# A hybrid decoder layer on one core: weight sums, row sums and sample sums of the feed-forward part put elsewhere

## The chip, the cores and the metric

The kernel runs on one core of a Trainium2 chip. The time is that of the device, in microseconds (us), of one execution; three executions of the kernel before took 2315.43, 2320.51 and 2323.57 us, so the median is 2320.51. The engines are named as in the profile: PE (matmuls), DVE (vector), ACT (activations), POOL (general), and SP, which here issues the transfers.

## The reference, cut to what matters

One decoder layer on 2048 prompt rows and 8 x 8 sample rows of 1024 features, in float32. The change touches its second half:

```python
mix = jnp.einsum('bte,ed->btd', jnp.concatenate([attn, gla_out], axis=-1), w_out)
x = x + rms_norm(mix, g_mix_post)
h = rms_norm(x, g_ffn_pre)
u = jax.nn.relu(jnp.einsum('btd,df->btf', h, w_up))      # 1024 -> 4096
f = jnp.einsum('btf,fd->btd', u * u, w_down)             # 4096 -> 1024
x = x + rms_norm(f, g_ffn_post)
```

The first half, the projections, the windowed attention and the gated linear attention, is the same in both kernels.

## The kernel before

Every float32 product is made of three matmuls: each operand is split into a high half (a rounding copy, on ACT) and a low half (the difference, on DVE), and high x high, high x low and low x high are summed in PSUM. The functions `split_by`, `split_up`, `split_sums` and `split_h` make such pairs.

The two feed-forward products are done by seven block products instead of eight (a Strassen-Winograd scheme over 2 x 2 blocks). One operand's blocks are summed over rows, the other's over weights: `H[1]` to `H[7]` are the pieces of the normed rows, and the weights' sums are made per chunk. A piece of 1024 rows is called `sb` (0 or 1); `up(g, before)` is one of 32 chunks (`g`; 0 to 15 for sb 0, 16 to 31 for sb 1) of 256 columns of `w_up`, and in it `p` is the product (1, 5, 7, 6, 3, 2, 4), where 0, 8 and 9 stand for the sample rows' matmuls in sb 0. In a chunk, `raw0` and `raw1` hold the weights as loaded, `w00`/`w01` and `w10`/`w11` their high and low halves, `t13` the weight sums, `s130`/`s131` and `s240`/`s241` the halves of the sums for products 5, 7 and for 6, 3. `sums_13` and `sums_24` each make two sums in `t13`. The products land in four PSUM banks, X (`ua`), Z (`uc`), Y (`ub`) and V (`ud` or `ue` in turn), and are combined into the seven slots of a tile `st` on DVE; ACT squares them (`squared`) and SP stores the tile in `s_d`. `end()` is the part of a chunk's combination that runs during the next chunk. `both` is ACT's copy of the sample rows' result, `fold` a matmul that adds its two halves.

Before the first chunk stands the out projection (line 1237), row block by row block in the order `B_ORDER`, whose last two are blocks 11 and 15. `residual` normalizes such a block, adds it to x, normalizes again, transposes (`xnT`), and for every pair of blocks makes the rows' sums (`ht`), which go through `h_d` in DRAM and come back as the pieces H (`fetch_h`). It is a generator: each `run(res, 1)` lets it go one step further at the place where that stands.

The feed-forward part has no scheduler: the order written in the code is the order of each engine (`ac`, `dv`, `te` and `sy` are wrappers that keep it, all their instructions being recorded at line 138). So a step that waits holds everything behind it on its engine.

Beside the chunks run sums of `w_down`'s blocks for the down projection (`load_down`, `sum_down`, at the places in `SUM_AT`, on DVE, stored in `t_d`). The down projection (`dn`) then reads `s_d` and `t_d` back as `os` and `ot`, splits them, and adds the banks of each product to `f` on DVE (`gather`); `gather_sample` does that for the sample rows (`dsam`, `fs`).

Of the kernel before, what the change touches and what calls it, by code (L numbers as in the profile page):

```python
# [52 lines left out]
SUM_AT = sorted([(g, 1) for g in range(1, NG) if not NFC - 3 < g <= NFC] + [(g, 4) for g in (18, 21, 24, 27)])  # L53
# [95 lines left out]
def hybrid_step_kernel(ctx: ExitStack, tc: tile.TileContext, I, O):  # L149
# [1184 lines left out]
    xsT = U["xs"].tile([P, KT, 2 * NS], F32R, tag="x", name="xsT", bufs=1)  # L1334
    open_pools(R, ("x",), "o")
# [13 lines left out]
    def load_x(i, sync=nc.sync):  # L1349
# [16 lines left out]
    def residual(i, banks, scalar=nc.scalar, vector=nc.vector, tensor=nc.tensor, sync=nc.sync, kinds=None):  # L1366
        n = rows(i)
        last = i in B_ORDER[-2:]
        x = res_x.pop(i, None) or load_x(i)[0]
        ssq = ends[B_ORDER.index(i) % 2]  # L1370
        pool, tag, bufs = (hs_pool, "h1", 1) if last else (R["x"], "x1", 2)
        x1 = pool.tile([P, D], F32, tag=tag, name=f"x1_{i}", bufs=bufs)
# [27 lines left out]
        if i < NB and not second and i:  # L1400
            sums_place(sb, j)
        for h in range(2):
# [8 lines left out]
            if i == NB:  # L1411
                split_copy(xsT[:, kk, :NS], xsT[:, kk, NS:], pt[:, :, :NS], vector)
                continue
            ht = sums[sb, j]
            scalar.activation(ht[:, (6, 2)[h] if second else h], pt, AF.Copy)
            if sb == 0 and not second:
                split_copy(H[h + 1][0][:, :, q], H[h + 1][1][:, :, q], pt, vector)
        yield
        if i == NB or not second:
            return  # L1420
# [55 lines left out]
    def sums_on(g):  # L1476
        return nc.gpsimd if g in (1, NFC, NFC + 1) else dv

    def sums_13(g):
# [3 lines left out]
        sums_on(g).tensor_tensor(t[:, :, 0], a21, a22, op=ALU.add)  # L1483
        sums_on(g).tensor_tensor(t[:, :, 1], a11, a21, op=ALU.subtract)

    def sums_24(g):
# [3 lines left out]
        sums_on(g).tensor_tensor(t[:, :, 0], t[:, :, 0], a11, op=ALU.subtract)  # L1490
        sums_on(g).tensor_tensor(t[:, :, 1], a12, t[:, :, 0], op=ALU.subtract)
# [17 lines left out]
    close_pools(R)  # L1509
    open_pools(U, ("sam", "s13h", "t13", "s13l", "s24h"), "u")  # L1510
    sums_13(0)
    split_sums(0, 13)
    sums_24(0)
# [14 lines left out]
    open_pools(U, ("s24l",), "u")  # L1528
    fetch_h(0, 5)
    fetch_h(0, 7)  # L1530
    run(res)
    fetch_h(0, 6)
    s_first = U["st0"].tile([P, 7, BT], F32, tag="st", name="st_0", bufs=1)
# [3 lines left out]
    load_up(1)  # L1537
# [449 lines left out]
```

## Time and profile before

| | before |
|---|---|
| median of three executions | 2320.51 us |
| profiled execution | 2319.51 us |
| its span in the trace | 2317.7 us |
| granted clock of TensorE, mean | 0.987 |
| PE / DVE / ACT / POOL busy | 96% / 69% / 52% / 13% |
| chain that ended last: PE / DVE / ACT | 71% / 16% / 6% |

A line of busy time names the engine, the operation, the tile written and the tiles read, and behind a bracket the idle time before it with what ended it. A window's line has the stretch in us, its length, the busy time of PE, of its weight loads, of DVE, ACT and POOL with the number of instructions in brackets, then the granted clock, the share of the DMA engines and GB/s. A line of waits has the engine, what it was about to do, what it waited for, the total in us, how often, and the longest. In the profile the out projection runs from 800 to about 976 us, the chunks to about 1655, and the down projection after that.

### The profile page before, as it was taken

The numbers are of one execution on the slowest core, as the hardware profiler recorded it, in microseconds if no ns is written. First come the engines' busy times: TensorE is split into PE (matmuls) and PEld (weight loads), VectorE is DVE, ScalarE is ACT, GpSimd is POOL, SyncE is SP. The second block draws the span as 40 slices with busy tenths as digits, with TensorE's granted clock in tenths as the row PEclk, the third lists the DMA queues.
The fourth block names the chain that finished last, engine by engine and source line by source line (L and its number), as shares of the span: only waits on it lengthen the run. The fifth ranks groups of instructions, "written<-read, shape, count | busy, mean of one in ns | idle before, by whom it ended". The sixth has DMA issues, their size and how long they took to land.

```text
span 2317.7 us, 34065 instructions
## 1 busy us (share of the span) xinstructions
PE 2224.0 (96%) x11800; PEld 1885.6 (81%) x11800; DVE 1609.6 (69%) x3331; ACT 1210.2 (52%) x2513; POOL 290.1 (13%) x440
## 2 busy tenths in 40 slices
PE   8999999999998899979999989999999999999997
PEld 7888887888887788858888878888888887888886
DVE  5888868787777666677677687777644555855557
ACT  5787755444554444445555565555444434554445
POOL 3566412111121101010000010000000000000000
PEclk9999999999999999989999999999999999999999
DMA  7343232121112355765545476666665755876665
GB/s 229 120 152 124 98 94 72 65 71 47 51 47 73 133 179 181 228 220 200 188 169 198 171 260 214 222 231 220 211 205 168 234 182 158 275 231 222 218 193 198
DMA packets 227266, 391.34 MB, mean 169 GB/s; under 512 B 22945, under 2 KB 134966, under 8 KB 223110
## 3 DMA queue, kind: packets, MB, share of 16 engines
q1 hardware_dynamic: 227094, 389.17, 50.0%
q8 instruction: 93, 1.52, 0.3%
q14 instruction: 79, 0.65, 0.1%
HBM read 254.56 MB, written 135.59 MB: 168 GB/s over the span
## 4 chain that ended last, share of the span: by engine, by line
PE 71%; DVE 16%; ACT 6%; issue 3%; DMA 2%; POOL 1%; DVEq 0%; SPq 0%; ACTq 0%; POOLq 0%
PE dn L138 25%; PE uc L138 7%; PE ua L138 7%; PE out L1237 7%; PE gproj L138 5%; PE ue L138 4%; PE ud L138 4%; PE ub L138 3%; DVE s L138 2%; PE proj L138 2%; DVE XQ L973 2%; PE sam L138 1%; PE dsam L138 1%; DVE pl L138 1%; PE gm L138 1%
## 5 line engine op out<-in xcount | busy, mean ns | idle before, releaser
L138 PE MATMUL dn<-ot,os 128*128 128x512 f32 x2688 | 625.0, 390 | 5.0 <-DVE f L138 2.9
L138 PEld LDWEIGHTS dn<-ot,os 128*128 128x128 f32 x2688 | 505.0, 188 | 114.5 <-DVE ot L138 4.7
L138 DVE TENSOR_TENSOR os<-os 128x512 fp32r<-128x512 f32 x224 | 154.7, 691 | 222.5 <-ACT os L138 221.7
L138 PE MATMUL gproj<-wg,gx 128*128 128x388 f32 x1408 | 289.3, 352 | 0.0
L138 ACT ACTIVATE os<-os 128x512 fp32r<-128x512 f32 x224 | 141.4, 631 | 281.1 <-DMA os<-s_d 218.9
L138 PEld LDWEIGHTS gproj<-wg,gx 128*128 128x128 f32 x1408 | 246.7, 192 | 13.5 <-issue 13.1
L138 ACT ACTIVATE st<-st 128x512 f32<-128x512 f32 x224 | 141.2, 630 | 141.9 <-DVE st L138 137.8
L138 PE MATMUL uc<-H,s 128*128 128x512 f32 x768 | 186.1, 391 | 2.0 <-ACT st L138 1.2
L138 PE MATMUL ua<-H,w 128*128 128x512 f32 x744 | 179.9, 390 | 0.9 <-DVE w L138 0.5
L138 PEld LDWEIGHTS uc<-H,s 128*128 128x128 f32 x768 | 144.7, 189 | 32.9 <-ACT st L138 1.7
L138 PEld LDWEIGHTS ua<-H,w 128*128 128x128 f32 x744 | 138.9, 188 | 30.1 <-DVE w L138 1.0
L138 DVE TENSOR_TENSOR st<-st 128x512 f32<-128x512 f32 x160 | 111.0, 694 | 69.4 <-ACT st L138 66.1
L1237 PE MATMUL out<-wo,mt 128*128 128x512 f32 x656 | 155.1, 395 | 3.3 <-DVE x L1387 3.3
L1237 PEld LDWEIGHTS out<-wo,mt 128*128 128x128 f32 x656 | 122.1, 188 | 30.9 <-issue 3.5
L214 POOL TENSOR_TENSOR frs<-rs_v,half 128x1 f32<-128x1 f32 (+1 forms) x13 | 9.0, 689 | 904.5 <-DVE rs_v L138 904.5
L138 ACT ACTIVATE s<-t 128x1024 fp32r<-128x1024 f32 x64 | 67.8, 1060 | 65.6 <-PE ue L138 26.6
L138 DVE TENSOR_TENSOR ot<-ot 128x512 fp32r<-128x512 f32 x128 | 88.2, 689 | 14.7 <-ACT ot L138 13.6
L138 PE MATMUL proj<-wa_hi,xh 128*128 128x384 f32 (+1 forms) x272 | 95.7, 355 | 0.9 <-ACT wa_hi L138 0.6
L138 DVE TENSOR_TENSOR s<-t,s 128x1024 fp32r<-128x1024 f32 x64 | 78.4, 1225 | 25.8 <-ACT s L138 22.5
L138 PE MATMUL proj<-wa_lo,xh 128*128 128x384 f32 (+1 forms) x272 | 94.3, 351 | 0.0
L138 PE MATMUL proj<-wa_hi,xl 128*128 128x384 f32 (+1 forms) x272 | 93.3, 347 | 0.0
L138 ACT ACTIVATE ot<-ot 128x512 fp32r<-128x512 f32 x128 | 80.7, 631 | 20.5 <-DMA ot<-t_d 16.9
(371 smaller groups left out, 4092.2 us busy)
## 6 DMA issues: line engine op xcount, KB each, us to landing
os<-s_d SPq DMA_DIRECT2D x224, 256.0 KB, 2.8
s_d<-st SPq DMA_DIRECT2D x31, 1792.0 KB, 9.0
raw<-in_w_up SPq DMA_DIRECT2D x64, 512.0 KB, 5.5
ot<-t_d SPq DMA_DIRECT2D x128, 256.0 KB, 3.7
rt<-in_w_down SPq DMA_DIRECT2D x96, 256.0 KB, 3.0
t<-in_w_down SPq DMA_DIRECT2D x64, 256.0 KB, 3.4
t_d<-t SPq DMA_DIRECT2D x32, 512.0 KB, 7.2
gx<-xt_d SPq DMA_DIRECT2D x28, 512.0 KB, 4.0
```

Of the source, the lines that this page charges most:

```text
L138: ins = call(*a, **k)
L214: nc.gpsimd.tensor_tensor(out, v[:n], e, op=ALU.pow)
L973: nc.vector.tensor_tensor(xq[rr, :, l, r, : n // 2].rearrange("p g (m b) -> p g m b", b=b), dr[rr], qr[rr], op=ALU.mult)
L1237: te.matmul(p_, x, w[:, cc], start=k + u == 0, stop=k == KT - 1 and u == len(products) - 1)
```

## The change

- **Chunk 0's weight sums.** They were made after the last pair's first block, in `t13`. Now they are made during the out projection, in place of the raw weights, four operations, and the halves for products 5 and 7 with them; the halves for 6 and 3 follow at product 2 of chunk 0.
- **Weight sums on POOL.** Chunks 1, 16 and 17 had them there (`sums_on`); now all chunks have them on DVE.
- **The last pair's row sums.** They are kept in tiles of 8 KB per partition and stored piece by piece, the last one in chunk 1. Row block 15's transposes stand behind product 3 of chunk 0. H6 is split at product 2 of chunk 0 (before at 8) and H3 at product 5 (before at 7).
- **Homes.** The two homes of the raw weights change places (`other`), and the load of chunk 2's weights stands at product 2 of chunk 0; it stood at the end of that chunk.
- **The change of rows** (chunks 15, 16, 17). The three row sums of the features, `rows_summed`, are put off to `end()` for chunks 0, 15 and 16, and the end of chunk 15 to the end of chunk 16. In chunks 1 and 17 the copies of X and Z stand at product 7.
- **Down sums** have other places (`SUM_AT`): none in chunk 1 or 17, two in every odd chunk from 19 to 29.
- **Down projection.** For products 5 and 3 the sample rows' gather stands behind the four blocks' gathers; it stood ahead.

```diff
-SUM_AT = sorted([(g, 1) for g in range(1, NG) if not NFC - 3 < g <= NFC] + [(g, 4) for g in (18, 21, 24, 27)])
+SUM_AT = sorted([(g, 1) for g in range(2, NG) if not NFC - 3 < g < NFC + 2] + [(g, 4) for g in range(19, 30, 2)])
...
-        last = i == B_ORDER[-2]
-        pool, tag, bufs = (hs_pool, "h0", 1) if last else (R["x"], "x", 2)
-        x = pool.tile([P, D], F32, tag=tag, name=f"bx_{i}", bufs=bufs)
+        x = R["x"].tile([P, D], F32, tag="x", name=f"bx_{i}", bufs=2)
...
+        if i == B_ORDER[-1]:
+            x1 = s_second[:, 4:6].rearrange("p a t -> p (a t)")
+        else:
+            x1 = hs_pool.tile([P, D], F32, tag=f"h{at % 2}", name=f"x1_{i}", bufs=1)
...
+        if pair:
+            sums[i] = t_place(0, [P, 2, BT], "ht_last") if second else s_second[:, 2:4]
...
+            if pair:
+                scalar.activation(sums[i][:, h], pt.rearrange("p k t -> p (k t)"), AF.Copy)
+                continue
...
+        if pair and second:
+            (a0, a1), (a6, a2) = ([sums[u][:, h] for h in range(2)] for u in B_ORDER[-2:])
+            ht = t_place(1, [P, 2, BT], "ht_sums")
+            for p, out, a, b in ((4, ht[:, 0], a6, a0), (6, ht[:, 1], a2, a6), (5, a6, a2, ht[:, 0]), (3, a2, a1, a6)):
+                vector.tensor_tensor(out, a, b, op=ALU.subtract)
+                sync.dma_start(h_d[sb][:, p, :, q], out.rearrange("p (k t) -> p k t", k=KT // 2))
+                if p == 5:
+                    yield
+            return
...
-        other = g > 1 and g % 2 == 0
+        other = g % 2 == 1
...
-    def sums_on(g):
-        return nc.gpsimd if g in (1, NFC, NFC + 1) else dv
...
-            res_x[B_ORDER[-2]] = load_x(B_ORDER[-2])[0]
+            (a11, a21), (a12, a22) = quarters(0)
+            halves_[0, 13] = [
+                U[f"s13{u}"].tile([P, KT // 2, 2, P], F32R, tag="s", name=f"s13{u}_0", bufs=1) for u in "hl"
+            ]
+            nc.vector.tensor_tensor(a22, a21, a22, op=ALU.add)
+            nc.vector.tensor_tensor(a21, a11, a21, op=ALU.subtract)
+            for n_, src in enumerate((a22, a21)):
+                split_by(nc.scalar, nc.vector, *(t[:, :, n_] for t in halves_[0, 13]), src)
+            nc.vector.tensor_tensor(a22, a22, a11, op=ALU.subtract)
+            nc.vector.tensor_tensor(a12, a12, a22, op=ALU.subtract)
...
-    sums_13(0)
-    split_sums(0, 13)
-    sums_24(0)
...
+                if g != NFC:
+                    next(before, None)
...
-                deque(before, 0)
-                if g != 1:
+                if g != NFC:
+                    deque(before, 0)
+                if g % NFC != 1:
...
+                if g == 1:
+                    run(res)
...
+                if g % NFC == 1:
                     ac.activation(s[:, 1], X, AF.Copy)
                     ac.activation(s[:, 3], Z, AF.Copy)
+                    for k in range(2):
+                        load_down(k + (g > 1) * first_sums)
...
+                load_up(1)
...
-                    run(res, 1)
-                    sums_13(1)
...
-                    split_sums(0, 24)
-                    run(res, 1)
+                    halves_[0, 24] = [
+                        U[f"s24{u}"].tile([P, KT // 2, 2, P], F32R, tag="s", name=f"s24{u}_0", bufs=1) for u in "hl"
+                    ]
+                    (_, _), (a12, a22) = quarters(0)
+                    for n, src in enumerate((a22, a12)):
+                        split_by(ac, dv, *(t[:, :, n] for t in halves_[0, 24]), src)
+                    load_up(2)
+                    split_h(6)
...
+        if g == NFC:
+            deque(before, 0)
+        def rows_summed():
+            dv.tensor_tensor(s[:, 6], s[:, 0], s[:, 6], op=ALU.subtract)
+            dv.tensor_tensor(s[:, 5], s[:, 3], s[:, 6], op=ALU.subtract)
+            dv.tensor_tensor(s[:, 4], s[:, 5], s[:, 0], op=ALU.add)
+
+        late = g in (0, NFC - 1, NFC)
+        if not late:
+            rows_summed()
...
+            if late:
+                rows_summed()
...
-                todo.append(gather_sample(p, f, sam))
             todo.extend(gather(sb, p, j, f, p_) for j, p_ in enumerate(banks))
             if sam is not None:
+                todo.insert(0 if p in (1, 2) else 4, gather_sample(p, f, sam))
```

DVE at the end of chunk 0 and the start of chunk 1. Before: the low halves of chunk 1's weights, the last pair's four row sums, the low halves of chunk 1's sums, three sums of features, the samples' part, and at last the first sums of chunk 2 (`t13_2`) and a down sum (`t_0`).

```order
L138 TENSOR_TENSOR w01_1_11251<-raw0_1_11051,w00_1_11250 128x1024
L138 TENSOR_TENSOR ht_1_3_11107<-ht_1_3_11107 128x512 x4
L138 TENSOR_TENSOR s131_1_11276<-t13_1_11232,s130_1_11275 128x1024
L138 TENSOR_TENSOR s241_1_11282<-t13_1_11232,s240_1_11281 128x1024
L138 TENSOR_TENSOR st_0_11041<-st_0_11041 128x512 x3
L138 TENSOR_TENSOR samp_0_11295<-samq_0_11294,samp_0_11295 128x2x64
L138 TENSOR_TENSOR st_0_11041<-st_0_11041,ud_0_11080 128x512
L138 TENSOR_TENSOR w11_1_11321<-raw1_1_11052,w10_1_11320 128x1024
L138 TENSOR_TENSOR st_0_11041<-st_0_11041 128x512
L138 TENSOR_TENSOR t13_2_11332<-raw0_2_11271,raw1_2_11272 128x4x128
L138 TENSOR_TENSOR t13_2_11332<-raw0_2_11271 128x4x128
L138 TENSOR_TENSOR t_0_11285<-t_0_11285 128x256 x4
```

Now, from the same low halves to the samples' part:

```order
L138 TENSOR_TENSOR w01_1_11243<-raw0_1_11118,w00_1_11242 128x1024
L138 TENSOR_TENSOR t13_1_11272<-raw0_1_11118,raw1_1_11119 128x4x128
L138 TENSOR_TENSOR t13_1_11272<-raw0_1_11118 128x4x128
L138 TENSOR_TENSOR s131_1_11276<-t13_1_11272,s130_1_11275 128x1024
L138 TENSOR_TENSOR ht_sums_11279<-ht_last_11246,st_1_11045 128x512
L138 TENSOR_TENSOR ht_sums_11279<-ht_last_11246 128x512
L138 TENSOR_TENSOR ht_last_11246<-ht_last_11246,ht_sums_11279 128x512
L138 TENSOR_TENSOR t13_1_11272<-t13_1_11272,raw0_1_11118 128x4x128
L138 TENSOR_TENSOR t13_1_11272<-raw1_1_11119,t13_1_11272 128x4x128
L138 TENSOR_TENSOR s241_1_11289<-t13_1_11272,s240_1_11288 128x1024
L138 TENSOR_TENSOR samp_0_11293<-samq_0_11292,samp_0_11293 128x2x64
L138 TENSOR_TENSOR st_0_11044<-st_0_11044,ud_0_11078 128x512
L138 TENSOR_TENSOR w11_1_11318<-raw1_1_11119,w10_1_11317 128x1024
```

Chunk 1's four weight sums (`t13_1`) have come onto DVE, and the three sums of features have gone.

DVE from chunk 16's first row piece (`H11_1`) on, while PE ends chunk 15. Before:

```order
L138 TENSOR_TENSOR H11_1_13757<-hraw_1_0_13667,H10_1_13756 128x1024
L138 TENSOR_TENSOR H11_1_13757<-hraw_1_1_13668,H10_1_13756 128x1024
L138 TENSOR_TENSOR st_15_13671<-st_15_13671,ub_15_13674 128x512
L138 TENSOR_TENSOR st_15_13671<-st_15_13671 128x512
L138 TENSOR_TENSOR st_15_13671<-st_15_13671,uc_15_13673 128x512
L138 TENSOR_TENSOR s241_16_13802<-t13_16_13703,s240_16_13801 128x1024
L138 TENSOR_TENSOR H51_1_13719<-H51_1_13719,H50_1_13718 128x1024 x2
L138 TENSOR_TENSOR H71_1_13736<-H71_1_13736,H70_1_13735 128x1024 x2
L138 TENSOR_TENSOR H61_1_13775<-H61_1_13775,H60_1_13774 128x1024 x2
L138 TENSOR_TENSOR st_15_13671<-st_15_13671 128x512 x3
L138 TENSOR_TENSOR samp_15_13869<-samq_15_13868,samp_15_13869 128x2x64
```

Now:

```order
L138 TENSOR_TENSOR H11_1_13757<-hraw_1_0_13667,H10_1_13756 128x1024
L138 TENSOR_TENSOR H11_1_13757<-hraw_1_1_13668,H10_1_13756 128x1024
L138 TENSOR_TENSOR st_15_13671<-st_15_13671,ub_15_13674 128x512
L138 TENSOR_TENSOR st_15_13671<-st_15_13671 128x512
L138 TENSOR_TENSOR t13_16_13703<-t13_16_13703,raw0_16_13528 128x4x128
L138 TENSOR_TENSOR t13_16_13703<-raw1_16_13529,t13_16_13703 128x4x128
L138 TENSOR_TENSOR st_15_13671<-st_15_13671,uc_15_13673 128x512
L138 TENSOR_TENSOR s241_16_13802<-t13_16_13703,s240_16_13801 128x1024
L138 TENSOR_TENSOR H51_1_13719<-H51_1_13719,H50_1_13718 128x1024 x2
L138 TENSOR_TENSOR H71_1_13736<-H71_1_13736,H70_1_13735 128x1024 x2
L138 TENSOR_TENSOR H61_1_13775<-H61_1_13775,H60_1_13774 128x1024 x2
L138 TENSOR_TENSOR samp_15_13866<-samq_15_13865,samp_15_13866 128x2x64
```

Two of chunk 16's weight sums (`t13_16`) have come in ahead of the halves `s241_16`, and three sums of chunk 15's features have gone from ahead of the samples' part (`samp_15`).

DVE in the down projection at the end of product 5 of sb 0, where the samples' bank (`dsam_5`) and the blocks' banks (`dn_0_5_0` and on) are added. Before:

```order
L138 TENSOR_TENSOR os_48_17245<-os_48_17245 128x512
L138 TENSOR_TENSOR ot_48_17246<-ot_48_17246 128x512
L138 TENSOR_TENSOR fs_16937<-fs_16937,dsam_5_16947 128x512
L138 TENSOR_TENSOR f_0_16940<-f_4_16557,dn_0_5_0_16943 128x512
L138 TENSOR_TENSOR os_49_17267<-os_49_17267 128x512
L138 TENSOR_TENSOR ot_49_17268<-ot_49_17268 128x512
L138 TENSOR_TENSOR f_1_16970<-f_5_16559,dn_0_5_1_16944 128x512
L138 TENSOR_TENSOR f_2_16973<-f_6_16561,dn_0_5_2_16945 128x512
```

Now:

```order
L138 TENSOR_TENSOR os_48_17253<-os_48_17253 128x512
L138 TENSOR_TENSOR ot_48_17254<-ot_48_17254 128x512
L138 TENSOR_TENSOR f_0_16948<-f_4_16565,dn_0_5_0_16951 128x512
L138 TENSOR_TENSOR f_1_16978<-f_5_16567,dn_0_5_1_16952 128x512
L138 TENSOR_TENSOR os_49_17275<-os_49_17275 128x512
L138 TENSOR_TENSOR ot_49_17276<-ot_49_17276 128x512
L138 TENSOR_TENSOR f_2_16981<-f_6_16569,dn_0_5_2_16953 128x512
L138 TENSOR_TENSOR f_3_17006<-f_7_16571,dn_0_5_3_16954 128x512
L138 TENSOR_TENSOR os_50_17299<-os_50_17299 128x512
L138 TENSOR_TENSOR ot_50_17300<-ot_50_17300 128x512
L138 TENSOR_TENSOR fs_16945<-fs_16945,dsam_5_16955 128x512
```

The samples' add has moved from ahead of the first block's add to behind the fourth.

More of the change, by code (lines that the diff above doesn't have):

```diff
@@ L1367, in residual @@
         n = rows(i)
-        last = i in B_ORDER[-2:]
+        at, pair = B_ORDER.index(i), i in B_ORDER[-2:]
         x = res_x.pop(i, None) or load_x(i)[0]
-        ssq = ends[B_ORDER.index(i) % 2]
-        pool, tag, bufs = (hs_pool, "h1", 1) if last else (R["x"], "x1", 2)
-        x1 = pool.tile([P, D], F32, tag=tag, name=f"x1_{i}", bufs=bufs)
+        ssq = ends[at % 2]
+        if i == B_ORDER[-1]:
+            x1 = s_second[:, 4:6].rearrange("p a t -> p (a t)")
+        else:
+            x1 = hs_pool.tile([P, D], F32, tag=f"h{at % 2}", name=f"x1_{i}", bufs=1)
         if i == NB:
@@ L1399, in residual @@
         q = slice(j * P, (j + 1) * P)
-        if i < NB and not second and i:
+        if pair:
+            sums[i] = t_place(0, [P, 2, BT], "ht_last") if second else s_second[:, 2:4]
+        elif i < NB and not second and i:
             sums_place(sb, j)
@@ L1417, in residual @@
                 split_copy(H[h + 1][0][:, :, q], H[h + 1][1][:, :, q], pt, vector)
+        if pair:
+            part = slice(2, 3) if second else slice(0, 2)
+            src = sums[i][:, 1:2] if second else sums[i]
+            sync.dma_start(h_d[sb][:, part, :, q], src.rearrange("p a (k t) -> p a k t", k=KT // 2))
         yield
-        if i == NB or not second:
+        if pair and second:
[7 more added lines that the diff above has]
+            return
+        if i == NB or not second or pair:
             return
@@ L1531, in hybrid_step_kernel @@
     run(res)
+    res_11 = residual(*early.pop(0), ac, dv, te, sy)
+    run(res_11, 3)
     fetch_h(0, 6)
-    s_first = U["st0"].tile([P, 7, BT], F32, tag="st", name="st_0", bufs=1)
+    s_first, s_second = (U[f"st{u}"].tile([P, 7, BT], F32, tag="st", name=f"st_{u}", bufs=1) for u in range(2))
     res_x[B_ORDER[-1]] = load_x(B_ORDER[-1], sy)[0]
@@ L1587, in up @@
         sb, fc = divmod(g, NFC)
-        s = U[f"st{g % 2}"].tile([P, 7, BT], F32, tag="st", name=f"st_{g}", bufs=1) if g else s_first
+        s = U[f"st{g % 2}"].tile([P, 7, BT], F32, tag="st", name=f"st_{g}", bufs=1) if g > 1 else (s_first, s_second)[g]
         first, more = g == 0, g + 1 < NG
@@ L1606, in up @@
             if p == 1:
-                next(before, None)
+                if g != NFC:
+                    next(before, None)
                 if g:
@@ L1660, in up @@
                     split_up(1, 0)
+                    run(res, 1)
             elif p == 8 and sb == 0:
```

40 lines of the change are left out of this document (15 added, 25 removed).

## The prediction

> **What bounds the kernel now.** I read the engines' busy time first, then the chain that ended last, then PE's waits, and last the stretches in which PE is not full.
>
> ```profile
> PE 2224.0 (96%) x11800; PEld 1885.6 (81%) x11800; DVE 1609.6 (69%) x3331; ACT 1210.2 (52%) x2513; POOL 290.1 (13%) x440
> PE 71%; DVE 16%; ACT 6%; issue 3%; DMA 2%; POOL 1%; DVEq 0%; SPq 0%; ACTq 0%; POOLq 0%
> ...
> PE xnT L138 <- DVE x L138: 6.5, 1, 6.5
> PE sam L138 <- ACT both L138: 7.5, 2, 5.3
> PE dn L138 <- DVE f L138: 2.9, 1, 2.9
> ...
> 950.00:1000.00 50.00, 43.50 (x216) 36.15 (x215) 35.89 (x47) 23.82 (x42) 6.99 (x8) 0.97 0.74 247
> 1000.00:1050.00 50.00, 41.74 (x174) 33.34 (x175) 32.57 (x47) 23.64 (x38) 2.57 (x2) 0.89 0.62 207
> 1300.00:1350.00 50.00, 47.76 (x216) 39.71 (x215) 33.55 (x38) 29.87 (x45) 9.86 (x6) 0.93 0.69 252
> 1350.00:1400.00 50.00, 46.44 (x197) 37.69 (x196) 39.90 (x54) 27.58 (x39) 3.27 (x2) 0.97 0.62 216
> 1450.00:1500.00 50.00, 50.00 (x223) 41.39 (x222) 39.88 (x62) 24.00 (x36) 0.00 (x0) 1.00 0.63 218
> 1900.00:1950.00 50.00, 50.00 (x222) 41.39 (x222) 24.03 (x37) 18.90 (x30) 0.00 (x0) 1.00 0.54 166
> 1950.00:2000.00 50.00, 47.12 (x202) 38.53 (x201) 37.52 (x55) 26.94 (x45) 2.74 (x5) 0.97 0.72 228
> ```
>
> PE bounds it: 96% busy, 71% of the chain. The windows give PE's busy time first, then PEld, DVE, ACT, POOL, and the granted clock. At 1450 and 1900 us PE is full at clock 1.00; there no side work can be worth anything. The change can only win where PE has holes: 950 to 1050 (A, the start of feed-forward), 1300 to 1400 (B, the change of rows) and 1950 to 2000 (C, the down projection). The waits name the holes. Since the matmuls stay the same in number, the sum is over holes and over matmuls at a reduced clock:
>
> ```profile
> 1030.00:1035.00 5.00, 0.61 (x3) 0.19 (x1) 4.34 (x7) 2.87 (x5) 0.00 (x0) 0.94 0.97 402
> 1035.00:1040.00 5.00, 4.08 (x12) 3.40 (x13) 2.94 (x5) 2.88 (x7) 0.00 (x0) 0.50 0.48 161
> 1340.00:1345.00 5.00, 3.19 (x10) 2.71 (x11) 3.50 (x3) 4.94 (x9) 3.37 (x2) 0.66 1.02 406
> 1955.00:1960.00 5.00, 3.86 (x10) 3.10 (x11) 5.00 (x9) 2.32 (x5) 0.00 (x0) 0.66 0.19 55
> ...
> 1341.81 1.11 PE L138 MATMUL sam<-fold,both 128*128 128x64 f32 x4 [2.24 <-ACT both L138]
> 1342.68 5.47 PE L138 MATMUL ue<-H,w 128*128 128x512 f32 x12
> 1353.66 2.88 PE L138 MATMUL ud<-H,s 128*128 128x512 f32 x12
> 1367.50 0.49 PE L138 MATMUL ud<-H,w 128*128 128x512 f32 x1 [2.79 <-ACT H L138]
> 1368.76 4.38 PE L138 MATMUL ud<-H,w 128*128 128x512 f32 x11 [0.76 <-DVE H L138]
> ```
>
> Each hole above 2 us is followed by matmuls at half clock: after the 2.24 us wait a product of 12 matmuls took 5.47 us where 2.88 is normal. A hole is thus paid about twice.
>
> **The change, part by part.**
>
> A. Before, the fold of chunk 1's sample rows (the 5.3 us wait) ends a chain on DVE and ACT, which starts at a transfer:
>
> ```profile
> 1017.85 6.79 DMA raw<-in_w_up
> ...
> 988.46 2.35 DVE L138 TENSOR_TENSOR H<-H,H 128x1024 fp32r<-128x1024 f32 x2
> 994.10 4.41 DVE L138 TENSOR_TENSOR H<-H,H 128x1024 fp32r<-128x1024 f32 x2 [0.20 <-ACT H L138]
> 995.18 2.25 POOL L1483 TENSOR_TENSOR t<-raw,raw 128x512 f32<-128x512 f32 x1
> 1003.33 0.03 DVE H L138
> ...
> 1017.47 1.23 DVE L138 TENSOR_TENSOR s<-t,s 128x1024 fp32r<-128x1024 f32 x1 [3.86 <-ACT s L138]
> 1024.73 0.69 DVE L138 TENSOR_TENSOR t<-raw,raw 128x512 f32<-128x512 f32 x1 [1.13 <-DMA raw<-in_w_up]
> 1025.94 1.80 DVE L138 TENSOR_TENSOR t<-t 128x256 f32<-128x256 f32 x4
> ...
> 1035.92 1.12 PE sam L138 x4
> ```
>
> Chunk 2's weights land at 1024.6, DVE starts their sums at 1024.73, and 11.2 us later the fold starts. The change issues that load at chunk 0's product 2, some 27 us earlier, so it binds no more: DVE's own queue does. H4's low half starts at 1003.33; before it stands the H3 pair, which took 4.41 us beside POOL's two weight sums and 2.35 without (988.46). POOL's sums go, 2.06 us come back, of which about 0.7 is lost to row 15's squares now standing in front of H4 on ACT: H4 starts at 1002.0. From H4 to the sums of chunk 2, DVE took 20.3 us before, 3.86 of them a wait for POOL's half of chunk 1's sums. Now there are four adds for chunk 1 on DVE itself (4 x 0.61, from 0.69 each less the overlap), and about 1.5 us of the wait returns as waits for ACT's high halves: 20.4 us. Chunk 2's sums then start at 1022.4 instead of 1024.7. Behind them 1.80 us of down sums go (SUM_AT no longer has chunk 1), but the fourth row sum of the last pair (0.61) and ACT's copy of Z behind it come in; I leave 11.2. The fold starts at 1033.6, a gain of 2.3. Everything PE does before is absorbed by that wait, since PE reaches the fold at about 1027: its product 3 now goes ahead of row 15's transposes (the 6.5 us hole), but the H3 and H4 splits come late in turn (holes of about 2.2 and 3.8 us), and chunk 1's low halves (2.4). These only move PE's idle time. The half clock behind the fold stays: 0.50 in its row. Bounds: if POOL's share does not come back and the adds stand on top, chunk 2's sums start at 1026.0 (a loss of 1.3); if none of the 3.86 us returns, at 1020.9 (a gain of 3.8).
>
> The sums made in place during the out projection: four adds and two 512-wide low halves, 6 x 0.61 = 3.7 us on DVE around 812 to 824.
>
> ```profile
> 812.00:824.00 12.00, 12.00 (x58) 9.78 (x57) 8.28 (x12) 5.42 (x11) 1.08 (x2) 1.00 0.43 165
> ```
>
> DVE is idle 3.7 of those 12 us and the stage runs on behind it, so they cost nothing; the bound is 3.7 once. Separate transfers for the last pair add five issues on SP, which has gaps of microseconds: nothing, at most one late load.
>
> B. The chain into the 2.24 us fold wait, and the tail behind it:
>
> ```profile
> 1332.16 4.54 DVE H L138 x2
> ...
> 1338.06 1.30 ACT L138 ACTIVATE st<-st 128x512 f32<-128x512 f32 x2 [5.21 <-DVE st L138]
> 1339.26 1.04 ACT L138 ACTIVATE s<-t 128x1024 fp32r<-128x1024 f32 x1
> ...
> s_d<-st SPq DMA_DIRECT2D x31, 1792.0 KB, 9.0
> ...
> s_d<-st SPq DMA_DIRECT2D x1, 1792.0 KB, 8.1
> ```
>
> H1's low halves take 4.54 us beside POOL; without it 2.35, so the squares at 1338.06 come 2.2 us earlier. Chunk 16's two sums now stand on DVE behind it, which holds ACT's high half of them to 1337.25 instead of 1339.26: 2.0 earlier, and so is the fold. The wait shrinks from 2.24 to about 0.3, and with it goes the half clock (5.47 less 2.88, and 0.5 in the fold, 0.3 in the next product: 3.3). The second hole stays: H4's high half is queued on ACT behind product 6's squares; by the order it starts at 1360.6 where PE wants it at 1359.3, a wait of 3.3 where it was 3.55 (2.79 + 0.76), and 1.74 of half clock behind it (4.38 less 11/12 of 2.88). The put-off work fills what was free: chunk 15's end and rows of both chunks stand behind product 2 of chunk 16. Gain 2.0 + 3.3 + 0.2 = 5.5. New is a wait of ACT: chunk 17's copies of X and Z go into the tile that chunk 15's s_d store reads, now issued at about 1369 instead of in chunk 16's first product. The median store lands after 9.0 us, the one issued between 1360 and 1390 after 8.1. Laid end to end, PE's product 3 of chunk 17 waits from 1377.7 and would get its bank 1.8 later at 9.0, 0.9 later at 8.1, at once below 7.2. I take nothing, since at 1369 no loads stand ahead of the store, and keep the wait as a rival. Bounds: 2 (the wait of 1.8 with 1.7 of clock) to 10.8 (2.24 + 3.3 + 3.55 + 1.74, both holes gone).
>
> C. Down projection, p = 5 and 3: the gather of the samples goes behind the blocks' gathers.
>
> ```profile
> 1951.25 0.69 DVE L138 TENSOR_TENSOR fs<-fs,dsam 128x512 f32<-128x512 f32 x1 [4.78 <-PE dsam L138]
> 1951.97 1.06 ACT L138 ACTIVATE fs_fold<-fs 64x1024 f32<-64x1024 f32 x1 [6.23 <-DVE fs L138]
> 1953.06 1.22 DVE L138 TENSOR_TENSOR fs<-fs,fs_fold 64x1024 f32<-64x1024 f32 x1 [1.12 <-ACT fs_fold L138]
> 1955.41 1.27 DVE L138 TENSOR_TENSOR f<-f,dn 128x512 f32<-128x512 f32 x2
> ```
>
> The block's adds, which free PE's banks, stand behind DVE's 4.78 us wait for the samples. Moved ahead they need only banks long finished: the 2.9 us wait goes, with 1.7 us of half clock (clock 0.66 over the 5 us from 1955). The samples' chain (0.69 + 1.12 + 1.22 = 3.0 us) now delays splits of the next units; DVE is half idle in this stage (24.03 of 50), so they are ahead of PE. Gain 4.6; bounds 0 to 4.6.
>
> The two more down sums after chunk 18 (1.80 each) lie under full PE: DVE goes from 80% to at most 86%. Nothing.
>
> Sum: 2.3 + 5.5 + 4.6 = 12.4. The profiled execution took 2319.51, 1.0 below the median 2320.51: 2307.1 on its scale, 2308 on the runs'.
>
> [...]
>
> **Rivals.**
> 1. The wait only moves. DVE in A is as late as before (gain 0, or -1.3), and s_d of chunk 15 lands after 9 us: B keeps 5.5 - 1.8 - 1.7 = 2.0. With C: 6.6, so 2314. For it: DVE at 72% in A takes over POOL's sums, and the median landing of s_d is 9.0. Against: POOL's sums slow DVE by nearly as much as they would take it.
> 2. All holes close: A's fold wait with its clock (5.3 + 2.5, clock 0.50 over 5 us), all of B (10.8), C (4.6): 23.2, so 2297. For it: DVE has idle time in both. Against: H4's place behind the squares.
> [...]
> 4. Slower: DVE falls behind in the second half. The six odd chunks from 19 to 29 with two down sums each leave PE a hole as the shortest here that cost its clock, 2.24 + 1.7: 6 x 3.94 = 23.6 against the 12.4, so 2332. It decides once a chunk's DVE work passes its PE time. Against: chunks 18, 21, 24 and 27 carry two now, and the window at 1450 shows PE at 50.00.
>
> **How the numbers follow.** Some 0.3%, 7 us, is what a measurement of this kernel can tell from no change: the bounds are 2313.5 and 2327.5. The forecast has 0.62, with its own range 2302 to 2313; rival 1 0.19, rival 2 0.07, rival 3 0.06, rival 4 0.06. Faster 0.62 + 0.07 + 0.06 = 0.75; same 0.19; slower 0.06. The range 2300 to 2317 leaves out rival 4, most of rival 2 and a piece of rival 1.
>
> **What would show it.** A: the fold of chunk 1 at about 1033.6 still waiting for ACT's copy (some 6 us, since PE comes earlier), no POOL rows at L1483 to L1491, and no wait of 6.5 before row 15's transposes. B: the first fold without a wait and at clock 1.00, `ud` of chunk 16 still waiting 3 us. C: no wait of dn for f near 1956. I am wrong if PE waits in chunk 17's third product, if the out projection shows a hole near 820, or if waits appear in the chunks from 19 on.

## The result and the profile after

The changed kernel took 2303.41 us in the median of four executions (2301.52 to 2306.40) beside 2319.86 for the kernel before: the ratio is 0.9931 with a 95% interval of 0.991 to 0.9953, so it is 11 to 21 us faster. Its profiled execution took 2306.40 us, the slowest of its four, with a span of 2304.6; the span of the kernel before was 2317.7. The traces thus compare over 13.1 us.

The page's lines of busy time and of the chain, then PE's longest waits behind the projections, and the windows that were shown of before, now of the changed kernel:

```profile
PE 2219.7 (96%) x11800; PEld 1882.1 (82%) x11800; DVE 1611.5 (70%) x3345; ACT 1209.4 (52%) x2515; POOL 271.2 (12%) x428
PE 69%; DVE 16%; ACT 7%; issue 5%; DMA 2%; POOL 1%; DVEq 0%; SPq 0%; ACTq 0%; POOLq 0%
...
PE ud L138 <- ACT H L138: 4.3, 2, 2.4
PE uc L138 <- ACT st L138: 3.7, 1, 3.7
PE dn L138 <- ACT ot L138: 2.3, 2, 1.5
PE sam L138 <- ACT both L138: 0.2, 1, 0.2
...
1000.00:1050.00 50.00, 42.98 (x178) 34.49 (x179) 36.31 (x50) 25.20 (x38) 0.00 (x0) 0.90 0.53 178
1300.00:1350.00 50.00, 49.80 (x239) 41.59 (x238) 36.07 (x43) 34.12 (x49) 0.00 (x0) 1.00 0.73 275
1350.00:1400.00 50.00, 47.37 (x201) 38.51 (x200) 40.69 (x57) 26.72 (x39) 0.00 (x0) 0.97 0.57 201
1950.00:2000.00 50.00, 50.00 (x222) 41.41 (x221) 39.53 (x56) 27.39 (x47) 3.14 (x6) 1.00 0.84 271
812.00:824.00 12.00, 12.00 (x58) 9.77 (x57) 10.70 (x18) 6.28 (x14) 1.40 (x2) 1.00 0.37 132
```

The waits of 6.5 (before row 15's transposes), 5.3 (fold) and 2.9 us (dn for f) are gone. PE is full, or within 0.2 us of it, at 1300 and 1950 us. Holes are left, some of them new: `uc` waits 3.7 us in chunk 1 for a copy of ACT, and `ud` waits for H4, 2.4 us in chunk 0 (no wait before) and 1.9 in chunk 16 (2.8 before). In the out projection DVE went from 8.28 to 10.70 of 12 us, and PE stayed full.

To see where the 13.1 us came from, I cut each trace at places that PE passes in both kernels: A is the stretch from the first matmul of the out projection to product 6 of chunk 2, B from product 6 of chunk 15 to that of chunk 18, D from the first `dn` to the last matmul of the sample rows, C from there to the last `dn`. Between them, chunks 2 to 15 and 18 to the end took 279.41 and 258.40 us in every run here. The column A2 is A without the out projection itself: from the first product of chunk 0 on.

| kernel | median, us | ratio to before, 95% | A | A2 | B | D | C |
|---|---|---|---|---|---|---|---|
| before | 2319.86 | | 250.5 | 74.6 | 70.0 | 292.2 | 356.1 |
| changed | 2303.41 | 0.9931 (0.991, 0.9953) | 246.1 | 70.2 | 63.9 | 294.8 | 351.0 |
| c_alone | 2316.39 | 0.9988 (0.9979, 0.9996) | 250.4 | 74.5 | 70.1 | 294.2 | 352.5 |
| c_undone | 2312.22 | 0.9962 (0.9949, 0.9974) | 248.0 | 69.5 | 63.3 | 294.7 | 357.3 |
| before_dve | 2317.28 | 0.9992 (0.9984, 1.0001) | 250.7 | 73.2 | 68.3 | 293.1 | 356.1 |
| after_pool | 2305.07 | 0.9933 (0.992, 0.9945) | 244.9 | 69.1 | 65.4 | 294.9 | 351.2 |
| load2_late | 2304.08 | 0.9928 (0.9914, 0.9942) | 247.2 | 69.7 | 63.9 | 293.5 | 351.7 |
| homes_undone | 2304.35 | 0.9939 (0.9926, 0.9953) | 245.4 | 69.5 | 63.9 | 293.5 | 353.7 |
| sum4_early | 2305.92 | 0.9943 (0.9931, 0.9956) | 247.3 | 71.5 | 63.2 | 293.9 | 352.4 |
| both_early | 2302.43 | 0.9925 (0.9912, 0.9937) | 244.2 | 68.4 | 63.2 | 293.5 | 351.2 |
| h4_early | 2306.68 | 0.9942 (0.9929, 0.9956) | 248.2 | 70.7 | 64.4 | 293.5 | 352.2 |
| h4_no_defer | 2300.84 | 0.9924 (0.9911, 0.9937) | 247.0 | 69.6 | 61.6 | 293.3 | 351.5 |
| best | 2302.28 | 0.9926 (0.9914, 0.9938) | 246.0 | 68.6 | 61.5 | 293.1 | 351.6 |
| best_pool1 | 2301.67 | 0.9921 (0.9908, 0.9934) | 244.6 | 66.2 | 61.6 | 293.1 | 351.6 |

Each ratio stands against runs of the kernel before on the same chip, so ratios compare across rows better than medians. Changed minus before: A 4.4, B 6.1, C 5.0 gained, D 2.5 lost, 0.4 gained ahead of the out projection and 0.2 lost behind the last `dn`; together the 13.1, within rounding.

Why A2 beside A: the out projection starts behind a hole of 3.27 us in every kernel, and takes 175.9 us where the granted clock stays full behind it, 177.5 where it is half for 3.41 us, and 178.5 where it is half for 6.83, whatever the edit. (It was 175.9 in the kernel before and in the changed one.) The five traces whose code in A is that of the changed kernel (changed, c_undone, homes_undone, h4_early, h4_no_defer) have A from 245.4 to 248.2, but A2 from 69.5 to 70.7: a difference in A2 that leaves this range is more than the spread among these five. Ahead of A the same part of the program ended between 793.4 and 800.4 us in these traces, which is why spans and medians tell less than the marks.

No run takes back chunk 0's weight sums, the place of row block 15's transposes or the pieces of the last pair's row sums by itself, so the gain in A is not split among them.

### The profile page after: what moved, and what is told of

It is laid out like the page before. It is cut to its first block, busy times and chain, and to the rows that moved or that the text cites. A ratio compares the mean times of both kernels' runs of the same rounds, so it can differ in the third digit from the quotient of the medians.

```text
span 2304.6 us, 34069 instructions
## 1 busy us (share of the span) xinstructions
PE 2219.7 (96%) x11800; PEld 1882.1 (82%) x11800; DVE 1611.5 (70%) x3345; ACT 1209.4 (52%) x2515; POOL 271.2 (12%) x428
## 4 chain that ended last, share of the span: by engine, by line
PE 69%; DVE 16%; ACT 7%; issue 5%; DMA 2%; POOL 1%; DVEq 0%; SPq 0%; ACTq 0%; POOLq 0%
PE dn L138 24%; PE uc L138 7%; PE ua L138 7%; PE out L1237 7%; PE gproj L138 4%; PE ue L138 4%; PE ub L138 4%; PE ud L138 4%; DVE s L138 2%; PE proj L138 2%; DVE XQ L973 2%; PE sam L138 1%; PE dsam L138 1%; PE gm L138 1%; DVE pl L138 1%
```

## The experiments

### Down projection: the gather alone, and the gather undone

`c_alone` is the kernel before with only this part, `c_undone` the changed kernel without it.

```diff
-                todo.append(gather_sample(p, f, sam))
             todo.extend(gather(sb, p, j, f, p_) for j, p_ in enumerate(banks))
             if sam is not None:
+                todo.insert(0 if p in (1, 2) else 4, gather_sample(p, f, sam))
```

> The kernel before with one part of the change alone: in the down projection the samples' gather stands behind the four blocks' gathers for products 5 and 3. Theory: the 2.9 us wait for f near 1956 and the half clock behind it go, nothing else changes: 4.6 to 5 us faster than the kernel before, about 2315. Rival (it needs the new homes of the loads): less than 2 us.

> The changed kernel with one part taken back: in the down projection the sample rows' gather stands ahead of the four blocks' gathers again, for products 5 and 3. Theory: PE's wait for f of 2.9 us comes back once, with a half clock behind it worth 1.7 us: 4.6 slower than the changed kernel. [...] Rival 2, the gain near 1950 us came from the homes of the loads and not from the gather: no wait for f, within 1 us of the changed kernel.

PE's timeline: the start of the row behind the hole in `c_undone`, and the first `dn` waits of `c_alone`:

```profile
1947.46 52.86 PE L138 MATMUL dn<-ot,os 128*128 128x512 f32 x225 [2.88 <-DVE f L138]
```

```profile
1675.30 0.50 PE L138 MATMUL dn<-ot,os 128*128 128x512 f32 x1 [1.47 <-ACT ot L138]
1814.22 0.50 PE L138 MATMUL dn<-ot,os 128*128 128x512 f32 x1 [0.27 <-ACT ot L138]
```

The 2.88 us wait is there with the old order and gone with the new, in both kernels and with either homes, and half clock follows it (granted clock 0.50 from 1947.40 to 1950.81 in `c_undone`). C is 3.6 us shorter in `c_alone` and 5.0 in the changed kernel than in the kernel before, and 6.2 longer in `c_undone` than in the changed kernel; 4.6 lies among them. All kernels that keep the part have C from 351.0 to 353.7, those without it from 356.1 to 357.3. By its interval `c_alone` gains 1 to 5 us (2316.39 beside 2318.49 on its chip), and `c_undone` loses some 4 to 9 (0.9962 against 0.9921 to 0.9943 for the kernels that keep the part and the rest of the change). `c_alone` gave 2 us back in D, at a wait of 1.47 for `ot` that the kernel before did not have in its trace. The mechanism is shown; neither rival holds.

### POOL and DVE

`before_dve` is the kernel before with the sums of chunks 1, 16 and 17 on DVE, `after_pool` the changed kernel with them on POOL.

```diff
     def sums_on(g):
-        return nc.gpsimd if g in (1, NFC, NFC + 1) else dv
+        return dv
```

> The kernel before with one part of the change alone: the weight sums of chunks 1, 16 and 17 on DVE, none on POOL. Theory (POOL and DVE hold each other up): the pairs of H low halves that took 4.41 and 4.54 us take 2.35, the fold of chunk 15 comes 2.0 us earlier with no half clock behind it (5.3 gained), and the fold of chunk 1 stays where it is, since the transfer of chunk 2's weights lands when it did: 2320 becomes about 2315. Rival (DVE is the bound there, 12 more adds of 0.61 us make it late): both folds wait longer than 5.3 and 2.2 us, 2320 or more.

> The changed kernel with the weight sums of chunks 1, 16 and 17 on POOL again. Theory: the low halves beside POOL's adds take some 4.5 us instead of 2.35, the fold of chunk 15 waits 2 us again with a half clock behind it, 5 to 7 us slower than the changed kernel. Rival (the sums put off made the change of rows shorter, POOL does no harm): within 1 us of the changed kernel and no wait at the fold of chunk 15.

The two low halves of H1, then the fold of chunk 15 and the products of chunk 16 that wait, in `before_dve`:

```profile
1330.07 2.35 DVE L138 TENSOR_TENSOR H<-hraw,H 128x1024 fp32r<-128x1024 f32 x2
...
1337.74 0.66 PE L138 MATMUL sam<-fold,both 128*128 128x64 f32 x4 [0.20 <-ACT both L138]
1353.45 3.04 PE L138 MATMUL uc<-H,s 128*128 128x512 f32 x12 [1.34 <-ACT st L138]
1362.98 0.80 PE L138 MATMUL ud<-H,w 128*128 128x512 f32 x1 [3.77 <-ACT H L138]
```

The same in `after_pool`, with POOL's adds beside it:

```profile
1319.84 1.68 POOL L1509 TENSOR_TENSOR t<-t,raw 128x512 f32<-128x512 f32 x1 [12.20 <-DVE s L138]
1321.59 2.15 POOL L1510 TENSOR_TENSOR t<-raw,t 128x512 f32<-128x512 f32 x1
1320.28 4.55 DVE L138 TENSOR_TENSOR H<-hraw,H 128x1024 fp32r<-128x1024 f32 x2
...
1329.93 0.66 PE L138 MATMUL sam<-fold,both 128*128 128x64 f32 x4 [2.24 <-ACT both L138]
1330.40 3.01 PE L138 MATMUL ue<-H,w 128*128 128x512 f32 x12
```

And the fold in the changed kernel:

```profile
1335.03 0.66 PE L138 MATMUL sam<-fold,both 128*128 128x64 f32 x4 [0.20 <-ACT both L138]
1335.49 3.02 PE L138 MATMUL ue<-H,w 128*128 128x512 f32 x12
```

The pair takes 2.35 us without POOL and 4.55 beside it, in both kernels, and the fold waits 0.20 or 2.24 accordingly: the chain is as I read it. Its price is not. `before_dve` gained 1.6 in B, not 5.3, since part of the wait came back in chunk 16: 1.34 for the copy of Z before product 3, where there was none, and 3.77 instead of 2.79 for H4 before product 4. Its ratio (interval 0.9984 to 1.0001) can't be told from no change. `after_pool` lost 1.5 in B and was shorter in A2 (69.1) than any of the five traces; its ratio cannot be told from that of the changed kernel. I had expected 5 to 7 us. The hole of 2.24 us had a product of 5.47 us behind it in the kernel before and one of 3.01 here.

### The load of chunk 2's weights

```diff
-                    load_up(2)
                     split_h(6)
...
             split_sums(1, 13)
             run(res, 1)
+            load_up(2)
             sums_24(1)
```

> The changed kernel with the load of chunk 2's weights issued at the end of chunk 0 again instead of at its product 2. Theory (this transfer set the end of region A before): the weights land some 7 us after an issue near 1014, chunk 2's sums on DVE start near 1024.7 instead of 1021.8, and PE's wait at product 3 of chunk 1 grows from 3.7 to 6 or 7 us: 2 to 3 us slower than the changed kernel. Rival (the load is hidden by DVE's queue either way): no wait of DVE for the transfer, same time.

SP's issues of the weights, of the kernel before and of this one (each row two transfers), and DVE's first sums of chunk 2 in this one:

```profile
1013.16 5.98 SPq L138 DMA_DIRECT2D raw<-in_w_up  x2
```

```profile
1012.81 1.47 SPq L138 DMA_DIRECT2D raw<-in_w_up  x2
...
1020.55 0.68 DVE L138 TENSOR_TENSOR t<-raw,raw 128x512 f32<-128x512 f32 x1
```

The rival holds. Issued at 1012.8 here and at about 989 in the changed kernel, the weights are there when DVE's queue comes to them at 1020.55, with no wait, and A2 is 69.7. In the kernel before, SP began the pair at nearly the same time, but its first issue alone took 4.6 us, so the second transfer went out only at 1017.85. What SP issued just ahead of the load, in the kernel before and in this one:

```profile
h_d<-ht SPq DMA_DIRECT2D x1, 1792.0 KB
```

```profile
h_d<-ht_sums SPq DMA_DIRECT2D x2, 256.0 KB
```

In the kernel before, the last pair's row sums all left in one store at 1012.54, behind which the load stood; from 1013.7 on the transfers ran at some 290 GB/s, at which 1792 KB take 6.3 us. The change stores them in pieces, of which three of 256 KB left in the 2 us ahead of this load. That the one large store made the load late is thus likely, but neither the pieces nor the exchange of the homes was tried by itself.

### Chunk 1: what the 3.7 us wait is worth

`sum4_early` does the last pair's fourth row sum at the end of chunk 0; `both_early` in addition lets ACT copy `both` before the splits and squares behind product 3.

```diff
             split_sums(1, 24)
+            run(res)
...
-                if g == 1:
-                    run(res)
```

```diff
+                if g != 1:
-                if more and not first:
+                    if more and not first:
                         split_sums(g + 1, 24)
-                squared(s[:, 6])
+                    squared(s[:, 6])
...
                 ac.activation(both, sam[:, :FC], AF.Copy)
+                if g == 1:
+                    split_sums(g + 1, 24)
+                    squared(s[:, 6])
```

> The changed kernel with the last pair's fourth row sum at the end of chunk 0 instead of in chunk 1 behind chunk 2's first weight sums, so that ACT's copy of Z in chunk 1 is free earlier. Theory (DVE's queue sets when the fold of chunk 1 can start, and PE's wait at product 3 only stands in front of it): the 3.7 us wait at product 3 goes, a wait of 5 to 6 us stands at the fold instead, at about the same time, and the half clock now falls behind the fold where it costs: no gain, up to 2 us slower. Rival (the copy of Z was the bound): the 3.7 us and their half clock are gained, 4 to 6 us faster than the changed kernel.

> As the one before, and in chunk 1 ACT's copy for the fold stands ahead of the high half of chunk 2's sums and the squares of product 3. Theory (with both out of the way PE is next held by the squares of X behind the same queue): no wait at product 3 nor at the fold of chunk 1, a wait of 1 to 2.5 us before product 1 of chunk 2, region A 3 to 5 us shorter than in the changed kernel. Rival (DVE is behind as a whole): the same 5 us stand a product later with their half clock, no gain.

PE's timeline of chunk 1: product 3 and the fold in the changed kernel, in `sum4_early`, and in `both_early`:

```profile
1024.38 5.49 PE L138 MATMUL uc<-H,s 128*128 128x512 f32 x12 [3.70 <-ACT st L138]
...
1033.77 0.55 PE L138 MATMUL sam<-fold,both 128*128 128x64 f32 x4
1034.13 3.01 PE L138 MATMUL ue<-H,w 128*128 128x512 f32 x12
```

```profile
1018.80 3.01 PE L138 MATMUL uc<-H,s 128*128 128x512 f32 x12 [0.35 <-ACT st L138]
1030.30 1.11 PE L138 MATMUL sam<-fold,both 128*128 128x64 f32 x4 [4.79 <-ACT both L138]
1031.17 4.52 PE L138 MATMUL ue<-H,w 128*128 128x512 f32 x12
```

```profile
1017.22 3.01 PE L138 MATMUL uc<-H,s 128*128 128x512 f32 x12 [0.33 <-ACT st L138]
1026.38 0.80 PE L138 MATMUL sam<-fold,both 128*128 128x64 f32 x4 [2.45 <-ACT both L138]
```

In `sum4_early` the wait moved to the fold, 4.79 us, and A2 is no shorter (71.5 beside 69.5 to 70.7): PE's 3.7 us at product 3 were not a bound, DVE's and ACT's queue behind them was. `both_early` shortens that queue as well. The fold still waits 2.45, where I had expected no wait, and none came before product 1 of chunk 2, where I had put it. A2 is 68.4, and 68.6 in `best` with the same code in A: 1 to 2 us shorter than in the five traces, not the 3 to 5 expected.

### H4 and the store of chunk 15's features

```diff
-H_NEXT = {..., (2, 1): 3, (2, 5): 2, (2, 6): 4}
+H_NEXT = {..., (2, 1): 3, (2, 5): 2, (2, 7): 4}
```

`h4_no_defer` also takes back what the change put off around the change of rows (the copies of X and Z in chunk 17 stay at product 7):

```diff
-                if g != NFC:
-                    next(before, None)
+                next(before, None)
...
-        late = g in (0, NFC - 1, NFC)
+        late = g == 0
```

> The changed kernel with the split of H4 of the second row piece at product 7 of chunk 16 instead of behind product 6's squares. Theory (store of chunk 15's features bounds next): the wait of 1.9 + 0.8 us before product 4 of chunk 16 and its half clock of 1.7 go, but ACT's copies in chunk 17 go on waiting for that store until about 1371, so PE waits some 3 us at product 3 of chunk 17: at most 1.5 us faster. Rival (the store is issued earlier too): 4.4 us faster, no wait at product 3.

> H4 early as in the one before, and nothing put off around the change of rows: chunk 15's and 16's row sums and chunk 15's end stand where they stood in the kernel before. Theory: five more DVE operations (3 us) ahead of H3 and H2, whose halves then come late; no wait for the store, but a wait of 1 to 3 us before products 3, 2 or 4 of chunk 16: within 2 us of the changed kernel. Rival (the putting off is what made room): the waits of the experiment with DVE sums in the kernel before come back, 3.8 us before product 4, some 4 us slower than the changed kernel.

The changed kernel: PE's product 4 of chunk 16, and ACT's copy of X in chunk 17, which waits for the store:

```profile
1356.70 0.50 PE L138 MATMUL ud<-H,w 128*128 128x512 f32 x1 [1.87 <-ACT H L138]
1357.96 4.38 PE L138 MATMUL ud<-H,w 128*128 128x512 f32 x11 [0.76 <-DVE H L138]
...
1371.16 0.60 ACT L138 ACTIVATE st<-ua 128x512 f32<-128x512 f32 x1 [5.20 <-DMA s_d<-st]
```

`h4_early`, the same places, and `h4_no_defer`:

```profile
1354.75 2.88 PE L138 MATMUL ud<-H,w 128*128 128x512 f32 x12
1372.02 4.54 PE L138 MATMUL uc<-H,s 128*128 128x512 f32 x12 [3.51 <-ACT st L138]
...
1370.88 0.60 ACT L138 ACTIVATE st<-ua 128x512 f32<-128x512 f32 x1 [5.23 <-DMA s_d<-st]
```

```profile
1345.03 3.04 PE L138 MATMUL uc<-H,s 128*128 128x512 f32 x12 [1.36 <-ACT st L138]
1351.51 2.81 PE L138 MATMUL ud<-H,w 128*128 128x512 f32 x11 [0.50 <-DVE H L138]
```

`h4_early` did what its theory said: the hole at product 4 is gone, and the same time is lost 17 us later, where product 3 of chunk 17 waits 3.51 us for a copy that waits for the store, its half clock included (4.54). With nothing put off, the store is early, the wait is gone, and two short holes without half clock remain: B is 61.6 instead of 63.9, the same in `best` and `best_pool1`. So once H4 stands early, the putting off costs 2.9 us in B (64.4 beside 61.6). With H4 late it may pay: `before_dve`, which puts nothing off and has DVE's sums, has 68.3 beside the changed kernel's 63.9, but the two differ in other parts too, so that is not shown.

### The homes of the down projection's loads, and the parts together

The change also exchanged homes of the down projection's loads `os` and `ot`. `homes_undone` gives the loads their old homes; `best` joins the edits of `both_early` and `h4_no_defer`; `best_pool1` adds POOL for the sums of chunk 1.

```diff
-        home, tag = ((("raw", "raw0"), ("xs", "x"), ("h", "h1"), ("bh", "w")), ...
+        home, tag = ((("h", "h0"), ("xs", "x"), ("raw", "raw0"), ("bh", "w")), ...
```

> The changed kernel with the homes of the down projection's loads in the order of the kernel before. Theory (the order of the homes makes the first loads late): the waits of dn for ot near 1665 and 1805 shrink from 0.4 to 1.5 us to at most 0.4, and the stretch from the first dn to the last sample matmul falls from 293.3 to 294.9 us to 292.2 to 293.1. Rival (the waits come from the transfers' own spread): both waits stay as they are.

> The changed kernel with the fourth row sum at the end of chunk 0, the fold's copy early in chunk 1, H4 split at product 7 of chunk 16, and nothing put off around the change of rows. Theory (the gains of the two regions add): region A 3 us and region B 2 us shorter than in the changed kernel, 2298 to 2299. Rival (the regions' gains were chance positions of the half clock): no faster than the changed kernel.

> As the one before, with the weight sums of chunk 1 alone on POOL. Theory (in chunk 1 DVE's queue is the bound, so each add taken off it brings the fold forward, while POOL's hold on DVE falls where DVE waits for ACT anyway): the wait at the fold of chunk 1 shrinks from 2.45 us to about 1, region A 1 to 2.5 us shorter. Rival (POOL stretches the low halves of H3 or H4 to 4.4 us as in the kernel before): 1 to 2 us longer.

`homes_undone` has D at 293.5, as most of the others; of the waits for `ot`, that near 1660 fell to 0.16, that near 1800 stayed at 0.73, so the theory held for one of the two. D lies between 292.2 and 294.9 over all kernels, and `c_alone`, whose code up to there is that of the kernel before, has 294.2 beside its 292.2. I take the 2.5 us to be spread of the transfers, for the larger part, which is not shown; why the wait near 1805 is 0.7 to 1.6 us in all variants of the changed kernel and 0.2 to 0.3 in those of the kernel before stays open.

`best` has B as hoped (61.5) and A2 at 68.6, 1.7 less than the changed kernel where 3 were hoped for; its ratio of 0.9926 and that of `best_pool1`, 0.9921, lie below the 0.9931 of the changed kernel but well inside its interval. In `best_pool1` the fold of chunk 1 waits 2.45 us; that wait did not shrink. Yet A2 is 66.2, 2.4 less than in `best`. The product behind the fold, in `best` and in `best_pool1`:

```profile
1028.95 4.58 PE L138 MATMUL ue<-H,w 128*128 128x512 f32 x12
```

```profile
1032.88 3.01 PE L138 MATMUL ue<-H,w 128*128 128x512 f32 x12
```

Of the 2.4 us, 1.6 are the half clock that this time did not follow the hole, and 0.8 an earlier fold. So chunk 1's sums on POOL did no harm here and may gain a little. Both kernels are faster than the kernel before; that they are faster than the changed kernel is not shown.

## Why the prediction was right, point by point

- **The size.** The sum was 12.4; the two profiled executions differ by 13.1, the medians by 16.5 with 11 to 21 in the interval. The direction and the three places were right, and 2303.4 lies in the likeliest case's own range. That 12.4 and 13.1 lie so near is in part luck: A gave 2.1 more than forecast, and D, which had no term, took 2.5.
- **A, 2.3 forecast, 4.4 found.** DVE's queue came out nearly as laid end to end: chunk 2's sums start at 1021.76 (1022.4 forecast). The step that failed is "The half clock behind the fold stays". I had ACT's copy of Z in the sum, but only as a link of the chain to the fold; PE itself waits for it, at product 3. So the 3.7 us hole and the product at half clock (5.49) fall in front of the fold, under DVE's queue, and the product behind the fold runs at full speed (3.01 where it was 5.05). That is 2.0 of the missing 2.1. The fold's own time, 1033.77 for the 1033.6 forecast, fits by luck: it was to wait for ACT's copy of `both`, but that copy ended at 1032.93, and PE came later, held by its own product 3. `sum4_early` shows the case that I had written: hole at the fold, half clock behind it (4.52). DVE's first sums of chunk 2, ACT's copy of Z and its copy for the fold, in the changed kernel:

```profile
1021.76 0.68 DVE L138 TENSOR_TENSOR t<-raw,raw 128x512 f32<-128x512 f32 x1
1023.73 0.60 ACT L138 ACTIVATE st<-uc 128x512 f32<-128x512 f32 x1 [3.86 <-issue]
1032.57 0.36 ACT L138 ACTIVATE both<-sam 128x256 f32<-128x256 f32 x1
```

- **The term for the load of chunk 2** rested on the place of the issue. `load2_late` shows that the place is worth nothing in the changed kernel; what held the load up in the kernel before was likely the store ahead of it.
- **POOL.** The stretch of the low halves (4.55 beside 2.35) and the 2.0 us at the fold of chunk 15 were right. As a price they were not: each way of adding or removing POOL's sums alone moved the ratio by 0.0008 or less, some 2 us.
- **B, 5.5 forecast, 6.1 found.** The fold waits 0.20 at full clock. H4's wait is 2.6 (1.87 + 0.76) where 3.3 was forecast, its half clock stayed (4.38).
- **The store of chunk 15** was forecast to cost nothing if it lands early. It did in this trace, with a margin of 0.8 us: ACT's copies end at 1372.2, PE's product 3 starts at 1373.07. But PE came so late because product 4 had run at half clock. In `c_undone`, `sum4_early`, `both_early` and `load2_late`, with the same code there and no half clock, it waits at product 3 of chunk 17 (0.6 to 1.3 us), which I had named as a sign of being wrong, and in `h4_early` 3.51. Taking nothing for this wait was right by the place of the half clock.
- **C, 4.6 forecast, 5.0 found**, and 3.6 and 6.2 in the two experiments.
- **The out projection and the down sums** cost nothing, as forecast: PE full from 812 to 824, and the same 228.48 us from product 6 of chunk 18 to that of chunk 30 in every run.
- **Not forecast:** D, 2.5 lost in this trace. The rivals: the first came true as a mechanism where PE came earlier to chunk 17, the second and the fourth did not.
- **"Each hole above 2 us is followed by matmuls at half clock"** was misread from the trace of the kernel before: its hole of 3.27 us ahead of the out projection was followed by full clock, 1.00 (first row and first windows of the last section). No row that the prediction shows carries the chance of 0.06 given to rival 3; in the runs, holes of 2.2 to 3.3 us had full clock behind them in some traces and half clock in others (last section).

## What to carry to other kernels

A hole of the bound engine is the place where lateness shows, not where it arises: closing the link that ends the wait moves the hole to the next thing that the late queue gates (`sum4_early`, `h4_early`), and only work taken out of, or moved behind, that queue makes it shorter. When such a chain is laid end to end, write down for each link whether the bound engine waits for it directly, since a hole before a forced wait is free and the same hole behind it is paid. Cut the traces at common marks before crediting an edit: stretches in which PE stayed full agreed to 0.01 us here, and cutting the out projection off A narrowed the spread from 2.8 to 1.2 us, so the marks tell single microseconds that medians don't.

## What the runs showed of the hardware that I had not expected

The same hole is followed by half clock in one run and not in another. The first 48 matmuls of the out projection, in the kernel before and in `c_undone`:

```profile
800.35 11.24 PE L1237 MATMUL out<-wo,mt 128*128 128x512 f32 x48 [3.27 <-DVE x L1387]
```

```profile
798.34 13.83 PE L1237 MATMUL out<-wo,mt 128*128 128x512 f32 x48 [3.27 <-DVE x L1388]
```

Product 4 of chunk 16 behind a hole of 1.88 + 0.76 us, in `c_undone`:

```profile
1356.94 0.50 PE L138 MATMUL ud<-H,w 128*128 128x512 f32 x1 [1.88 <-ACT H L138]
1358.20 2.79 PE L138 MATMUL ud<-H,w 128*128 128x512 f32 x11 [0.76 <-DVE H L138]
```

It took 2.79 us here and in `load2_late`, `sum4_early` and `both_early`, but 4.38 in the changed kernel and 4.07 in `homes_undone`, whose code there is the same. The 2.24 us hole at the fold gave 5.47 before and 3.01 in `after_pool`. And where product 4 was not slowed, PE came earlier to chunk 17 and waited there for the store (1.32 us in `load2_late`), so B ended nearly the same.

What differs is where the hole falls. In all fourteen traces every change of the granted clock lies on one grid of 3.41 us. Windows of this grid around the 3.27 us hole, in the kernel before and in `c_undone`:

```profile
795.48:798.89 3.41, 1.60 (x10) 1.09 (x8) 1.67 (x5) 0.69 (x2) 0.02 (x1) 1.00 1.01 410
798.89:802.30 3.41, 1.95 (x9) 1.64 (x10) 2.63 (x3) 0.14 (x1) 0.53 (x1) 1.00 0.07 28
```

```profile
793.70:797.11 3.41, 1.37 (x9) 0.90 (x7) 1.67 (x5) 0.69 (x2) 0.25 (x1) 1.00 1.02 396
797.11:800.52 3.41, 2.18 (x5) 1.82 (x6) 2.63 (x3) 0.37 (x1) 0.30 (x1) 0.50 0.13 52
```

The hole leaves PE 1.60 and 1.95 us busy in its two windows before, and 1.37 in the first window of `c_undone`, which is followed by half clock. Over the fourteen traces from 600 us on, each window at full clock in which PE was busy less than 1.49 us was followed by half clock, and none with more than 1.72; the smaller matmuls ahead of that have exceptions. PE was not idle for the whole of the window that half clock followed in `c_undone`, but busy for 1.37 us of it, and behind holes of 2.2 to 2.6 us half clock came in some traces. The mean granted clock moved with the time from one execution of the changed kernel to the next: 0.992 at 2301.5 and 2302.0 us, 0.990 at 2304.8, 0.989 at 2306.4. The same hole stands at another place of the grid in another trace (PE busy for 1.60 or 1.37 us of its first window, above), so I reckon half clock behind a hole of 2 to 3 us as a chance times a price; that is an estimate.
